# Moving sums, squares and scales of an encoder block's branch, output and attention stages

## The chip, the core and the metric

The kernel runs on one core of a Trainium2 chip. The core has five engines, each with its own queue of instructions that it works through in order: TensorE (PE, matrix products), VectorE (DVE), ScalarE (ACT), GpSimd (POOL) and SyncE (SP, which here only issues DMAs). An engine stops at an instruction whose inputs or buffers are not ready, and everything behind it in that queue stops too. The metric is the time of one launch in microseconds, as the median of several runs.

## The reference

The program is one block of a bidirectional encoder on 1024 tokens of width 1024, in float32:

```python
h = layer_norm(x, ln0_g, ln0_b)
proj = h @ w_in + b_in
qa, ka, va, qb, kb, vb, ga, gb = split(proj)
y_na  = neighbourhood_attention(qa, ka, va, rpb) @ w_branch_na    # 8 heads of 64
y_swa = windowed_gqa_with_sink(rotary(qb), rotary(kb), vb, sink) @ w_branch_swa
mixed = sigmoid(ga) * y_na + sigmoid(gb) * y_swa
h = layer_norm(ALPHA * h + mixed @ w_out + b_out, ln1_g, ln1_b)
u = square(relu(h @ w_ff1 + b_ff1))                               # width 4096
h = layer_norm(ALPHA * h + u @ w_ff2 + b_ff2, ln2_g, ln2_b)
```

The neighbourhood attention looks at a window of 8 rows by 16 columns on a 16 by 64 grid, the windowed one at 128 positions to each side, with a sink logit in the denominator.

## The kernel before

**Planes.** PE works in float16. Every operand of a large product is held as two float16 planes, a high one (the scaled value rounded) and a low one (what the rounding left). A product is the sum of three: high times high, high times low, low times high. So that the planes use the range of float16, each weight matrix and activation is scaled by a power of its own sum of squares. Such a scale takes a chain over four engines: ACT squares and accumulates (`square_sum`, `wo_square`, `b_square`, `mx_square`, `squares1`), PE adds the 128 partial sums with a tiny product against ones (`total_of` at L193, `wo_scale` at L1400, `mx_scale` at L1482, `sum_sq1`), DVE bounds the sum, POOL raises it to a power. Then ACT writes the high plane and DVE the low one (`b_split`, `wo_split`, `split_mx`, `head_hi` and `head_lo`).

**Stages**, by the time in the profile of before:

- 0 to 48 us: layer norm 0 in eight groups of 128 tokens (`ln0_norm`), transposition through PE (L385), evacuation as planes (`ln0_turn`), and the first gate projections (L429).
- 48 to 95 us: projections. Work on the weights of coming chunks is put into a list with `defer(n, ...)`, and `flush` issues those pieces whose n products have passed; `pump(n)` issues n projection products. The plan's four numbers per chunk say after how many products each part of a chunk's weight work is due.
- 95 to 393 us: 64 attention steps (`steps`). A step issues the scores of step s + 2 (`part_a`, whose first score bank is `score_ps[0]`, and DVE's reduction at L781), the low plane and the DMA transposition (pt) of step s + 1 (`part_l`), the exponential (`part_e`) and the products with the values (`part_c`, L887). Between them it pumps projection products in three parts, 12 in all per step up to about 217 us and 18 later. The sums of a weight chunk are written beside the scores, into `score_ps[0]` (`total_bank`). `evac2` adds the second half of a head's output on DVE.
- 393 to 463 us: the remaining gates in a scheme of seven block products (L1174), with `o_hi` and `o_lo` making the planes of the attention output (L1276, L1278).
- 463 to 556 us: the branch stage. For f from 0 to 7 and for each half of the tokens, `branch(f, half)` runs two groups of twelve products (neighbourhood, then windowed) into two PSUM tiles, DVE multiplies each with a gate, and POOL adds the two into `mx`. Around it, the next weights are loaded, squared, scaled and split, and two gates a half are loaded by SP and put through a sigmoid on ACT.
- 556 to 655 us: output products. For each group g of 128 tokens `out_mm` runs 24 products for each half of the width (L1610 to L1612), `out_evac` adds the residual, `ln1_norm` normalises, `turn` transposes it through PE (L1640), `turn_evac` and `combine` make the planes for the next stage. `late(g)` scales and shifts late residuals on POOL (zl, L1792). `head_w`, `squares1`, `sum_sq1`, `scale1`, `head_hi` and `head_lo` get the first weights of the next stage ready (hS, tw).
- 655 to 949 and 949 to 1240 us: the two layers of the MLP (L1779, L2255), seven block products each.

**What sets the order.** The program is a manual schedule: each engine's queue is what the program text issues to it, in the order of the text. Moving a call moves all its instructions on every engine. Each PSUM tag (mm, s, t, o) has two tiles.

Of the kernel before, what the change touches and what calls it, by code (L numbers as in the profile page):

```python
# [70 lines left out]
NO_DVE = ()  # L71
# [4 lines left out]
N_PRE = 188  # L76
WARM = 18, 4, 4, 2, 0, 2
# [15 lines left out]
def encoder_block(ctx, tc, x, w_in, w_br, w_out, w_ff1, w_ff2, par, rows, rpbp,  # L93
# [623 lines left out]
    def plan():  # L717

        def to(j, n):
            return lambda: got[j].to(n)  # L720
        ev = []
        for j in range(1, len(todo)):
            u = 48 * j
            t = (u - 112, u - 84, u - 44, u - 28) if j > 8 else \
                [200 + 40 * (j - 7) + x for x in (0, 24, 44, 64)] if j > 6 else \
                [20 * j - 24 + x for x in ((0, 14, 30, 34) if j > 1 else (0, 10, 24, 28))]
            if j > 8:
                ev.extend((u - 152 + 6 * x, 0, (j, x)) for x in range(4))
            elif j > 2:
                ev.append((max(20 * (j - 3) + 12, 2) + (30 if j > 6 else 0), 0, (j, None)))  # L730
            ev.extend((x, n, j) for x, n in zip(t, (1, 3, 4, 5)))
        for x, n, j in sorted(ev, key=lambda e: e[0]):
            if n == 0:
                defer(x, lambda j=j: fetch(*j))
            else:
                defer(x, to(j, n), pe=n == 3, only=n != 3)
# [124 lines left out]
    def part_c(s):  # L861
# [26 lines left out]
        if t % 2 == 1:  # L888

            oo = oT[o_row:o_row + 64, o_chunk, (t // 2) * 512:(t // 2 + 1) * 512]  # L890

            def evac():
                ACT.copy(oo, po[64:P, :])

            def evac2():
                DVE.tensor_tensor(out=oo, in0=po[0:64, :], in1=oo, op=ALU.add)  # L896
            if s == 63:
                last_evac.extend((evac, evac2))
            else:
                evac()  # L900
                if t == 3 and o_row == 64:
                    defer(14, evac2, 2, lambda: norm(o_chunk))
                else:
                    defer(14, evac2)
# [31 lines left out]
    with tc.manual_schedule(engines=MANUAL):  # L936
# [110 lines left out]
        def steps(s, n, before_b=None, before_c=None):  # L1047
# [21 lines left out]
            if s >= C_LAG:  # L1069
                part_c(s - C_LAG)  # L1070
            flush()
            pump(part[2])
# [334 lines left out]
        def wo_split(k):  # L1407
# [13 lines left out]
                9: ((b_split, 0),), 10: ((b_scale, 1),)}  # L1421
# [10 lines left out]
        for n, (p, i) in enumerate(gseq[2:], 2):  # L1432
# [13 lines left out]
            if n in (4, 5, 6, 7, 10, 11):  # L1446
# [3 lines left out]
                o_lo(n_o)  # L1450
                n_o += 1
        b_split(1)
# [26 lines left out]
        def mx_scale(half, ps, ones_, pw_):  # L1479
            DVE.tensor_reduce(out=mtot[:, half:half + 1], in_=msq[:, 8 * half:8 * half + 8], axis=mybir.AxisListType.X,  # L1480
                              op=ALU.add)
            PE.matmul(ps[:, 0:2], ones_, mtot[:, half:half + 1].to_broadcast([P, 2]), start=True, stop=True)  # L1482
# [29 lines left out]
        def branch(f, half, between=None):  # L1512
            both = []
            for gi, (act, tag) in enumerate(((o_na, "t"), (o_swa, "o"))):
                ps = psum(tag)
                gemm3(ps, bws[f], lambda part, k: act(part, k, half), nk=4, k0=4 * gi)
                if gi == 0 and between:
                    between()
                s_ = sg[f, gi, half]
# [8 lines left out]
        for f in range(8):  # L1528
            for half in range(2):
# [6 lines left out]
                else:  # L1536
                    if f + 2 < 8:
                        wo_load(f + 2)
                    if f + 1 < 8:
                        wo_scale(f + 1)  # L1540
                        if f:
                            b_split(f + 1)
# [4 lines left out]
                if half == 0:  # L1547
                    if f + 1 < 8:
                        wo_square(f + 1)
# [4 lines left out]
                branch(f, half, (lambda: mx_scale(0, psum("s"), ones_b, pwb)) if (f, half) == (7, 1) else None)  # L1554
# [3 lines left out]
        split_mx(0)  # L1558
# [45 lines left out]
    def out_mm(g, n, k0, k1):  # L1604
# [3 lines left out]
        ps, (mh, ml) = pss[g, n], mhl[g]  # L1608
        for k in range(k0, k1):
# [186 lines left out]
    with tc.manual_schedule(engines=MANUAL):  # L1796
# [10 lines left out]
        for g in range(NCG):  # L1807
# [5 lines left out]
            out_evac(g, 0)  # L1813
            out_mm(g, 1, 0, 4)
            if g:
                turn(g - 1)
            if g == 7:
# [17 lines left out]
            if g == 5:  # L1835
                head_split(0, 1)
                head_split(0, 2)
            if g == 6:
                for p in range(2, 4):
                    squares1(p, raws[p])  # L1840
            out_evac(g, 1)
            ps = bound_sum() if g == 0 else None
            ln1_norm(g)
            if g == 0:
                bound(ps)
            if g == 1:
                mx_scale(1, psum("o"), ones, pw)
# [702 lines left out]
```

## Time and profile before

| what | us |
|---|---|
| median of 3 runs | 1252.29 (1251.12 to 1252.44) |
| profiled execution | 1251.06 |
| its span | 1249.2 |
| PE busy in it | 1215.4 |
| DVE, ACT, POOL busy | 970.9, 870.9, 339.2 |

The span runs from the first to the last instruction of the core; the profiled execution's own time is 1.9 us longer. A row of the view of waits names the waiting engine, the tile and line of the waiting instruction, and the instruction that ended the wait. In rows of the timeline, the brackets hold the idle time of the engine just before, with its releaser. In the views a tile's name stands for all its buffers: `bc<-raw` at L1396 is `wo_square`, `mx` at L1523 is the sum of two gated halves, `sn` at L1881 the evacuation of the first MLP layer.

### The profile page before, as it was taken

To read this page: it belongs to the slowest core of one execution; us is meant where nothing else is said; L and a number is where in the kernel's file an instruction comes from. 1 tells how busy PE (TensorE), PEld (TensorE's weight loads), DVE (VectorE), ACT (ScalarE), POOL (GpSimd) and SP (SyncE) were. 2 spreads that over 40 slices of the span, in tenths; PEclk is the share of its full clock that TensorE was granted. 3 is DMA by queue.
4 is the path that set the end of the run, shared out by engine and by line. 5 is a ranking of instruction groups with operands and counts; after the bars stand their busy time and mean duration, and the time that the engine had idled before them with its cause. 6 is when DMAs were issued, how large, how long until landed. Compare 5 with 4: busy or idle time off the path is not lost.

```text
span 1249.2 us, 17241 instructions
## 1 busy us (share of the span) xinstructions
PE 1215.4 (97%) x6070; PEld 607.5 (49%) x6070; DVE 970.9 (78%) x1416; ACT 870.9 (70%) x1417; POOL 339.2 (27%) x368
## 2 busy tenths in 40 slices
PE   7999999999999998999999999999999999999997
PEld 5545555555555443444544444444444444444443
DVE  6788998878887974554678887877857777898888
ACT  7569889999876477753557877787776746344447
POOL 5202223434320014556621013432300002211207
PEclk9999999999999998999999999999999999999999
DMA  8654668686756335526333457776636635363333
GB/s 321 192 183 120 152 150 173 160 189 152 157 148 187 109 132 179 192 91 246 118 135 110 151 179 259 238 234 243 207 113 256 219 135 227 126 261 127 127 110 135
DMA packets 177878, 216.84 MB, mean 174 GB/s; under 512 B 111744, under 2 KB 125312, under 8 KB 171136
## 3 DMA queue, kind: packets, MB, share of 16 engines
q1 hardware_dynamic: 176816, 214.89, 54.2%
q8 instruction: 47, 0.77, 0.3%
q10 hardware_dynamic: 976, 0.87, 0.2%
q14 instruction: 39, 0.32, 0.1%
HBM read 130.69 MB, written 59.33 MB: 152 GB/s over the span
## 4 chain that ended last, share of the span: by engine, by line
PE 82%; ACT 7%; DVE 6%; issue 2%; DMA 2%; POOL 1%; POOLq 0%; SPq 0%; ACTq 0%; DVEq 0%
PE ps_mm L429 17%; PE ps_t L1779 6%; PE ps_o L1779 6%; PE ps_mm L2255 6%; PE ps_s L2255 6%; PE ps_mm L1779 6%; PE ps_t L2255 5%; PE ps_o L2255 5%; PE ps_s L1779 2%; PE ps_o L887 2%; PE ps_o L1174 2%; PE ps_mm L1174 1%; PE ps_t L1174 1%; PE ps_t L419 1%; PE ps_o L419 1%
## 5 line engine op out<-in xcount | busy, mean ns | idle before, releaser
L429 PE MATMUL ps_mm<-hT 128*128 128x512 f16 x960 | 226.4, 379 | 4.2 <-DVE hT L398 2.0
L1779 PEld LDWEIGHTS <-tw 128*128 128x128 f16 x1248 | 122.0, 99 | 146.0 <-issue 1.9
L2255 PEld LDWEIGHTS <-hS 128*128 128x128 f16 x1008 | 98.7, 98 | 118.2
L429 PEld LDWEIGHTS <-hT 128*128 128x128 f16 x960 | 90.6, 99 | 101.5 <-issue 12.0
L800 ACT ACTIVATE ss<-ss,sk 128x384 f32<-128x384 f32 (+1 forms) x128 | 73.8, 578 | 25.1 <-DVE sk L781 24.8
L1779 PE MATMUL ps_t<-hS,tw 128*128 128x512 f16 x384 | 88.1, 379 | 1.2 <-ACT sn L1881 1.1
L1971 DVE TENSOR_TENSOR usl<-usl 128x512 f32<-128x512 f32 x64 | 51.5, 804 | 23.5 <-ACT usl L1899 23.3
L429 PE MATMUL ps_mm<-hT,wpair 128*128 128x512 f16 x288 | 68.8, 380 | 0.0
L1700 POOL TENSOR_TENSOR c<-c 128x2 f32<-128x2 f32 x16 | 15.5, 974 | 194.7 <-DVE c L1699 194.7
L2275 POOL TENSOR_TENSOR acc<-acc,rst 128x512 f32<-128x512 f32 x16 | 31.8, 1986 | 122.7 <-DMA rst<-xr_d 114.8
L200 POOL TENSOR_TENSOR hT<-hT 128x2 f32<-128x2 f32 x30 | 25.2, 840 | 117.7 <-DVE hT L199 117.7
L2088 DVE SCALAR_TENSOR_TENSOR hS<-stg,c,hS 128x2048 f16<-128x2048 f32 x21 | 50.0, 2379 | 7.6 <-ACT hS L2085 7.6
L1706 DVE SCALAR_TENSOR_TENSOR tw<-raw,c,tw 128x512 f16<-128x512 f32 x60 | 51.8, 864 | 5.1 <-ACT tw L1703 4.8
L2255 PEld LDWEIGHTS <-hA 128*128 128x128 f16 x336 | 32.9, 98 | 39.6
L1174 PEld LDWEIGHTS <-hT 128*128 128x128 f16 x336 | 32.8, 99 | 39.6 <-issue 1.1
L887 PE MATMUL ps_o<-pt,vv 128*128 128x256 f16 (+1 forms) x448 | 49.1, 250 | 1.5 <-DVE oT L896 0.8
L812 DVE SCALAR_TENSOR_TENSOR pl<-ss,pl 128x768 f16<-128x768 f32 (+1 forms) x42 | 46.6, 1110 | 0.9 <-ACT pl L803 0.7
L887 PEld LDWEIGHTS <-vv 128*128 128x128 f16 x448 | 35.5, 98 | 18.6 <-DVE oT L896 2.0
L1779 PE MATMUL ps_o<-hS,tw 128*128 128x512 f16 x192 | 44.0, 379 | 0.0
L1703 ACT ACTIVATE tw<-raw,c 128x512 f16<-128x512 f32 x60 | 41.7, 708 | 2.8 <-DVE raw L1744 2.8
L1523 POOL TENSOR_TENSOR mx<-sg 128x512 f32<-128x512 f32 x16 | 30.1, 1881 | 49.8 <-DVE sg L1521 23.8
L587 POOL TENSOR_TENSOR bm<-tb,mk 128x128 f32<-128x128 f32 x56 | 42.9, 796 | 0.7
(431 smaller groups left out, 3082.2 us busy)
## 6 DMA issues: line engine op xcount, KB each, us to landing
us_d<-usl SPq DMA_DIRECT2D x112, 256.0 KB, 3.1
stg<-us_d SPq DMA_DIRECT2D x28, 1024.0 KB, 4.8
raw<-in_w_ff SPq DMA_DIRECT2D x24, 512.0 KB, 5.6
sg<-sg_d SPq DMA_DIRECT2D x32, 256.0 KB, 2.8
hA<-in_w_ff SPq DMA_DIRECT2D x8, 1024.0 KB, 7.6
hS<-in_w_ff SPq DMA_DIRECT2D x8, 1024.0 KB, 7.8
hT<-in_w_in SPq DMA_DIRECT2D x60, 128.0 KB, 2.5
hT<-in_w_in SPq DMA_DIRECT2D x11, 512.0 KB, 4.6
```

Of the source, the lines that this page charges most:

```text
L429: PE.matmul(ps, a[:, k, :], act(b, k), start=(k == 0 and i == 0), stop=(k == NK - 1 and i == 2))
L587: bias_ops.append(lambda o=o, g0=g0, m=m, g=g: POOL.tensor_tensor(out=bm[:, o + g * P:o + (g + 1) * P].rearrange("p (a c) -> p a c", c=8), ...
L800: ACT.activation(p, p, AF.Exp, bias=nm[:, i:i + 1], scale=-1.0, accum_out=sums_l[o_chunk][:, hh, 2 * t + i:2 * t + i + 1])
L812: DVE.scalar_tensor_tensor(out=pl[:, n:2 * n], in0=e[:, 0:n], scalar=P_SCALE, in1=pl[:, 0:n], op0=ALU.mult, op1=ALU.subtract)
L887: PE.matmul(o, vs, move(part), start=(m == 0 and part == 0), stop=(m == len(runs) - 1 and part == 1))
L1174: PE.matmul(ps, w[:, a, k, :], act[:, b, k, :], start=(first and k == 0 and m == 0), stop=(k == 3 and m == 2), skip_group_check=True)
L1703: ACT.activation(hi_lo(slot, 0), src, AF.Copy, bias=0.0, scale=w_scale(p))
L1706: DVE.scalar_tensor_tensor(out=hi_lo(slot, 1), in0=src, scalar=w_scale(p), in1=hi_lo(slot, 0), op0=ALU.mult, op1=ALU.subtract)
L1779: PE.matmul(ps, ww, act[:, part, k, :], start=(first and k == 0 and m == 0), stop=(k == 3 and m == 2), skip_group_check=True)
L1971: DVE.tensor_tensor(out=out, in0=a, in1=b, op=op)
L2088: DVE.scalar_tensor_tensor(out=slot[:, :, 1, :], in0=src, scalar=scale, in1=slot[:, :, 0, :], op0=ALU.mult, op1=ALU.subtract)
L2255: PE.matmul(ps, st[:, a, part, j * P:(j + 1) * P], w[:, a, wpart, :], start=(first and a == 0 and m == 0), stop=(a == 3 and m == 2), skip_ ...
```

## The change

Eight places are edited; no arithmetic is added or removed except that two normalisations go to another engine.

1. `NO_DVE` holds 2 and 3: the normalisations of two groups of layer norm 0 run on DVE, not on ACT.
2. In the projections' plan the weight sums are due 18 products after their start, not 14.
3. In an attention step the deferred list is emptied of what needs no PE before the last pumped products, and of the rest after them; before, all of it was emptied ahead of them. `evac2` is due after 12 products, not 14 (`D_E2`).
4. `wo_square(1)` is issued in the stage before the branch stage. `wo_scale(f + 1)` is issued between the two groups of products of `branch(f, 1)`, not before them, and `b_split(f + 1)` therefore ahead of it. `o_lo(6)` and `o_lo(7)` are issued after their loop.
5. `split_mx(0)` is issued inside the last branch, ahead of its second gate product, and the first output products run all those with the high plane of the activation first.
6. The sum over `msq` for the second half of `mx` and its scale are issued inside group 1 of the output stage, not at its end.
7. In group 6 the two `squares1` come after the normalisation, not before.

```diff
-NO_DVE = ()
+NO_DVE = 2, 3
+D_E2 = 12
...
-                [20 * j - 24 + x for x in ((0, 14, 30, 34) if j > 1 else (0, 10, 24, 28))]
+                [20 * j - 24 + x for x in ((0, 18, 30, 34) if j > 1 else (0, 10, 24, 28))]
...
-                    defer(14, evac2)
+                    defer(D_E2, evac2)
...
                 part_c(s - C_LAG)
+            flush(False)
+            pump(part[2])
             flush()
-            pump(part[2])
...
-                9: ((b_split, 0),), 10: ((b_scale, 1),)}
+                9: ((b_split, 0),), 10: ((b_scale, 1),), 11: ((wo_square, 1),)}
...
                 o_hi(n_o)
-                o_lo(n_o)
+                if n < 10:
+                    o_lo(n_o)
                 n_o += 1
+        o_lo(6)
+        o_lo(7)
...
+        def mx_sum(half):
             DVE.tensor_reduce(out=mtot[:, half:half + 1], in_=msq[:, 8 * half:8 * half + 8], axis=mybir.AxisListType.X,
                               op=ALU.add)
+
+        def mx_scale(half, ps, ones_, pw_):
+            if half == 0:
+                mx_sum(0)
...
                 if gi == 0 and between:
                     between()
+                if (f, half, gi) == (7, 1, 1):
+                    split_mx(0)
...
-                    if f + 1 < 8:
-                        wo_scale(f + 1)
-                        if f:
-                            b_split(f + 1)
+                    if f and f + 1 < 8:
+                        b_split(f + 1)
...
-                    if f + 1 < 8:
+                    if 2 <= f + 1 < 8:
                         wo_square(f + 1)
...
-                branch(f, half, (lambda: mx_scale(0, psum("s"), ones_b, pwb)) if (f, half) == (7, 1) else None)
+                branch(f, half, None if half == 0 else (lambda f=f: wo_scale(f + 1)) if f < 7 else
+                       (lambda: mx_scale(0, psum("s"), ones_b, pwb)))
...
-        split_mx(0)
         split_mx(1)
...
+        if (g, n) == (0, 0):
+            for k in range(8):
+                for x in range(2):
+                    PE.matmul(ps, mh[:, k, :], wo[:, x, k, ns], start=(k + x == 0), stop=False)
+            for k in range(8):
+                PE.matmul(ps, ml[:, k, :], wo[:, 0, k, ns], start=False, stop=(k == NK - 1))
+            return
...
             out_evac(g, 0)
+            if g == 1:
+                mx_sum(1)
             out_mm(g, 1, 0, 4)
             if g:
                 turn(g - 1)
+            if g == 1:
+                mx_scale(1, psum("o"), ones, pw)
...
+            out_evac(g, 1)
+            ps = bound_sum() if g == 0 else None
+            ln1_norm(g)
             if g == 6:
                 for p in range(2, 4):
                     squares1(p, raws[p])
-            out_evac(g, 1)
-            ps = bound_sum() if g == 0 else None
-            ln1_norm(g)
...
-            if g == 1:
-                mx_scale(1, psum("o"), ones, pw)
```

How the queues change is shown at three places; the change's lines have moved by up to 18, and a number behind "x" counts equal instructions in a row. The first is ACT's queue where the branch stage starts. `bc<-raw` is `wo_square`, `bc<-braw` is `b_square`, `wb` is a high plane of branch weights, `sg` are sigmoids and `wo` a high plane of output weights. Before:

```order
L1246 ACTIVATE go<-ps_mm,hT 128x512
L1278 CAST oS<-oT 128x1024
L1388 ACTIVATE wb<-braw,bc 128x1024
L1508 ACT_TABLE_LOAD
L1508 ACTIVATE sg<-sg,prm 128x512 x2
L1409 ACTIVATE wo<-raw,bc 128x1024
L1508 ACTIVATE sg<-sg,prm 128x512 x2
L1396 ACTIVATE bc<-raw 128x1024
L1374 ACTIVATE bc<-braw 128x1024
```

With the change:

```order
L1248 ACTIVATE go<-ps_mm,hT 128x512
L1398 ACTIVATE bc<-raw 128x1024
L1280 CAST oS<-oT 128x1024
L1390 ACTIVATE wb<-braw,bc 128x1024
L1517 ACT_TABLE_LOAD
L1517 ACTIVATE sg<-sg,prm 128x512 x2
L1411 ACTIVATE wo<-raw,bc 128x1024
L1517 ACTIVATE sg<-sg,prm 128x512 x2
L1376 ACTIVATE bc<-braw 128x1024
```

The square of wo(1) has gone ahead of the last plane of the attention output.

The second is PE's queue at one attention step: the products with the values (L887), the sum of a weight chunk (`ps_s<-hT`) and the four pumped products, of which the first is shown. Before:

```order
L887 LDWEIGHTS vv
L887 MATMUL ps_o<-pt,vv 128x256
L193 MATMUL ps_s<-hT 128x2
L429 LDWEIGHTS wpair
L429 MATMUL ps_mm<-hT,wpair 128x512
```

With the change, from the last of the four on:

```order
L430 LDWEIGHTS wpair
L430 MATMUL ps_mm<-hT,wpair 128x512
L194 MATMUL ps_s<-hT 128x2
L780 MATMUL ps_s<-kh,q 128x384
L781 MATMUL ps_s<-kl,q 128x384
```

The sum now stands behind the four products and right ahead of the next scores.

The third is ACT's queue in group 6 of the output stage. `z<-z,mv` is the normalisation, `junk<-hS` are the two `squares1`, the casts into hS are high planes from `combine`. Before:

```order
L1651 ACTIVATE mx<-ps_t,c_5477 128x128 x6
L1689 ACTIVATE junk,c_5477<-hS_6064 128x2048
L1689 ACTIVATE junk,c_5477<-hS_6065 128x2048
L284 ACTIVATE z<-z,mv 128x1024
L1656 CAST hS_6065<-s2t 128x4x128
```

With the change:

```order
L1667 ACTIVATE mx<-ps_t,c_5477 128x128 x6
L285 ACTIVATE z<-z,mv 128x1024
L1705 ACTIVATE junk,c_5477<-hS_6064 128x2048
L1705 ACTIVATE junk,c_5477<-hS_6065 128x2048
L1672 CAST hS_6065<-s2t 128x4x128
```

The normalisation passes both squares; the casts keep their place behind them.

More of the change, by code (lines that the diff above doesn't have):

```diff
@@ L901, in part_c @@
                 if t == 3 and o_row == 64:
-                    defer(14, evac2, 2, lambda: norm(o_chunk))
+                    defer(D_E2, evac2, 2, lambda: norm(o_chunk))
                 else:
-                    defer(14, evac2)
+                    defer(D_E2, evac2)
     def fills():
@@ L1477, in mx_square @@
                            saturate=False)
-        def mx_scale(half, ps, ones_, pw_):
+        def mx_sum(half):
             DVE.tensor_reduce(out=mtot[:, half:half + 1], in_=msq[:, 8 * half:8 * half + 8], axis=mybir.AxisListType.X,
                               op=ALU.add)
+        def mx_scale(half, ps, ones_, pw_):
+            if half == 0:
+                mx_sum(0)
             PE.matmul(ps[:, 0:2], ones_, mtot[:, half:half + 1].to_broadcast([P, 2]), start=True, stop=True)
```

## The prediction

> **What bounds the kernel now.** I read the page's first lines, then everything that TensorE (PE) waits for, and last the stretches around its longest waits.
>
> ```profile
> span 1249.2 us, 17241 instructions
> PE 1215.4 (97%) x6070; PEld 607.5 (49%) x6070; DVE 970.9 (78%) x1416; ACT 870.9 (70%) x1417; POOL 339.2 (27%) x368
> ```
>
> PE is busy for 97% of the span, and the change removes none of its products. So only the 33.8 us in which PE is not busy, and time in which it is busy at a lower clock, can move. The view of waits (engine, operation and line, what released it: total us, times, longest) names the holes:
>
> ```profile
> PE ps_s L1400 <- ACT bc L1396: 4.3, 1, 4.3
> PE ps_s L193 <- DVE sk L781: 2.8, 3, 1.2
> PE ps_t L1640 <- ACT z L284: 2.1, 1, 2.1
> PE ps_o L1482 <- DVE prm L1480: 2.1, 1, 2.1
> PE ps_mm L1612 <- DVE m L1495: 1.6, 1, 1.6
> PE ps_o L887 <- DVE oT L896: 0.8, 1, 0.8
> PE ps_o L887 <- DMA pt<-hT: 0.7, 1, 0.7
> PE ps_t L193 <- ACT hT L222: 0.7, 1, 0.7
> PE ps_o L385 <- ACT ln L368: 0.2, 1, 0.2
> ```
>
> The edits touch the work around all of these. Windows (length, busy time and instruction count of PE, PEld, DVE, ACT and POOL, then granted clock, DMA share, GB/s) show where a hole also cost clock, and how full VectorE (DVE) is in attention:
>
> ```profile
> 125.00:150.00 25.00, 23.76 (x145) 14.46 (x144) 23.37 (x44) 19.52 (x40) 6.35 (x9) 1.00 0.65 159
> 150.00:175.00 25.00, 23.81 (x147) 14.35 (x144) 22.96 (x44) 20.87 (x48) 7.76 (x11) 1.00 0.62 146
> 217.00:393.00 176.00, 176.00 (x1016) 101.84 (x1015) 142.26 (x287) 150.26 (x294) 60.93 (x76) 1.00 0.67 158
> 470.00:475.00 5.00, 1.94 (x6) 1.01 (x7) 2.76 (x4) 4.97 (x9) 1.48 (x2) 0.73 0.70 245
> 475.00:480.00 5.00, 5.00 (x15) 1.87 (x14) 0.75 (x1) 3.47 (x6) 0.78 (x2) 0.59 0.63 210
> 650.00:655.00 5.00, 5.00 (x22) 2.74 (x21) 4.93 (x9) 3.53 (x9) 0.00 (x0) 0.68 0.26 105
> ```
>
> **The branch stage: the largest term.** The chain of waits (start us, length us, what) into the 4.3 us hole reads, with a stretch of undisturbed products ahead of it for the pace:
>
> ```profile
> 96.22 2.60 PE ps_mm L429 x12
> ...
> 470.65 1.32 ACT sg L1508 x2
> 471.97 1.05 ACT bc L1396 x2
> 473.06 0.59 PE ps_s L1400 x2
> ```
>
> The wait is for wo_square(1) (bc at L1396), queued on ScalarE (ACT) behind the sigmoids of loaded gates and a weight split. It now stands before the stage, so this release is gone; and wo_scale(f+1) goes in after the twelve products of one half instead of ahead of them. Behind the hole the clock cost 5 × (1 − 0.73) + 5 × (1 − 0.59) = 3.4 us of full-speed time; about 0.4 of it fell into the hole itself, so 3.0 were paid. Undisturbed, a product takes 2.60 / 12 = 0.216 us. Gross gain 4.3 + 3.0 = 7.3 us.
>
> [...]
>
> What is late next is ACT itself (start, length, operation, and idle before it with its releaser):
>
> ```profile
> 480.07 1.06 ACT L1396 ACTIVATE bc<-raw 128x1024 fp8e5<-128x1024 f32 x1 [1.13 <-DMA raw<-in_w_out]
> 484.80 0.63 ACT L1476 ACTIVATE bc<-mx 128x512 fp8e5<-128x512 f32 x1 [2.40 <-POOL mx L1523]
> 485.46 1.15 ACT L1388 ACTIVATE wb<-braw,bc 128x1024 f16<-128x1024 f32 x1
> ```
>
> With PE 7.3 us earlier, these do not all follow: the load of raw(2) stays where it was (its buffer is freed by a split behind the same loads), so wo_square(2) still starts near 480.1; behind it stand another such square (to 482.4), that of mx(0,1) (0.63), and the high plane of wb(2) (1.15), to 484.3; its low plane on DVE takes some 1.3 us more (the splits at L1495 below), to 485.6. PE starts f = 2 at 468.8 + 3 × 24 × 0.216 = 484.4 (three halves after the hole's beginning, 473.06 − 4.27), and wants that plane at its third product, 484.8. I take a new wait of 0.8 us, from 0 to 1.5 (the row's length either way). Net −6.5, range −7.3 to −5.8.
>
> **Attention.** The sums (L193) write beside the scores of the current step, so they wait until DVE has reduced those scores:
>
> ```profile
> 142.10 0.61 DVE L781 CUSTOM_DVE_ANT_0 ss<-ps_t,bd,snk 128x384 f32<-128x384 f32 x1
> ```
>
> Moving them behind the step's last four pumped products gives 4 × 0.216 = 0.86 us of cover. The two waits of 1.2 fall to 0.4, the third (2.8 − 2 × 1.2 = 0.4) vanishes: −2.1. The release of evac2 (the 0.8 us at L896) by 12 products instead of 14 falls into the step before, which takes that wait away. Against this, all pieces that an emptying of the deferred list issues (scale pieces on DVE and POOL, ACT splits, weight loads on SP) now stand in front of the next step's scores rather than in the middle of the step, on a DVE that is 94% and 92% busy in these windows. PE already waited 0.7 us for a transposed probability tile (pt), which comes at the end of a chain through DVE; a DVE piece of 0.5 to 0.8 us in front of a reduction makes some pt that much later. I take one or two such waits, +0.7. Net −2.2; from −3.6 (everything goes) to +3 (five new waits of the size seen, 1.2 us, against the whole gain of 2.9). The shift of the weight sums in the projections by 14 to 18 products covers 4 × 0.216 = 0.86, more than the 0.7 us at L193 ps_t: −0.7.
>
> **Layer norm.** Two normalisations go from ACT to DVE:
>
> ```profile
> L366 DVE TENSOR_SCALAR ln<-ln,mv x1: 814/814/814, 12.4 to 12.4; 128x1024 f32<-128x1024 f32 x1
> 28.37 1.24 ACT L368 ACTIVATE ln<-ln,mv 128x1024 f32<-128x1024 f32 x1
> 28.97 0.69 DVE L398 TENSOR_TENSOR hT<-t,hT 128x512 f16<-128x512 f32 x1
> ```
>
> On ACT the last ended at 29.6, just as PE came for it (the 0.2 us wait). On DVE it stands behind the low plane that ends at 29.66, so it ends near 30.45: +0.8, less a little because ACT, relieved of 2.5 us, evacuates earlier: +0.7, from −0.5 to +1.0.
>
> **First output products.** The 1.6 us wait at L1612 is for the low plane of m:
>
> ```profile
> 557.42 3.48 DVE L1495 SCALAR_TENSOR_TENSOR m<-mx,mxc,m 128x1024 f16<-128x1024 f32 x2
> ```
>
> The chain of waits gives the first of these two splits 1.3 us. Sixteen high-plane products first are 16 × 0.216 = 3.5 us of cover: −1.6. The last gate product of the branch on DVE (0.6 to 0.8 us) now stands behind the first split, and so, later by that, do POOL's last sum of two gates, ACT's last square and what SP loads behind it; I found no use of them that is due within 3 us, and if there is one the gain is smaller by 0.7. From −1.8 to −1.0.
>
> **The output stage.** Here I do not credit the waits. The 2.1 us at L1482 is taken off PE, but the next stretches hang on GpSimd (POOL):
>
> ```profile
> 583.15 0.71 POOL L1485 TENSOR_TENSOR mxc<-mxc,c 128x2 f32<-128x2 f32 x1
> 583.82 12.03 POOL L1792 TENSOR_TENSOR zl<-zl 128x512 f32<-128x512 f32 x8
> 596.03 0.55 POOL L1629 TENSOR_TENSOR mv<-mv,mhalf 128x1 f32<-128x1 f32 x1 [0.18 <-DVE mv L1628]
> ```
>
> Twelve microseconds of late residual work start behind mv(1) and end where mv(2) is wanted; I take it that each group's normalisation then follows the one before at POOL's pace as far as transposition 5, since four more additions stand between each two. What leaves POOL's path is the power for mxc, 0.7 us, which now runs in POOL's idle time before mv(1). So PE gains 2.1 and waits 1.3 of it later: −0.8.
>
> ```profile
> 635.76 0.83 PE ps_t L1640 x7
> 636.59 9.38 DMA hS<-in_w_ff
> 648.06 1.13 ACT z L284
> 690.87 2.75 PE ps_t L1779 x12
> ```
>
> The rows of POOL and ACT ahead of z:
>
> ```profile
> 644.24 0.35 POOL L282 TENSOR_SCALAR mv<-mv 128x1 f32<-128x1 f32 x1
> 643.56 1.91 ACT L1689 ACTIVATE junk<-hS 128x2048 fp8e5<-128x2048 f32 x1 [3.74 <-DMA hS<-in_w_ff]
> 646.05 1.91 ACT L1689 ACTIVATE junk<-hS 128x2048 fp8e5<-128x2048 f32 x1 [0.49 <-DMA hS<-in_w_ff]
> ```
>
> In this chain no PE work stands between 636.59 and 690.87: a load started by transposition 5, the squares of what it brings, z, then ACT and DVE pieces end to end. Moving the squares behind z removes the wait at L1640, but both squares are still ahead of the next casts. The first had run while its data came in (from 643.56); now it starts after z, whose scale POOL has ready at 644.6, so near 644.6 + 1.1 = 645.7. Two of 1.9 end near 649.6, and the casts start 0.4 later than at 648.06 + 1.13 = 649.2. The sums of squares on PE then wait about 2 us in place of the transposition. For 690.87 that is about +0.5, and the clock dip at 650 stays. Both together −0.3; if all of it were PE's, 2.1 + 2.1 + 1.6 of clock = −5.8.
>
> **Sum.** −6.5 − 2.2 − 0.7 + 0.7 − 1.6 − 0.3 = −10.6 us. The profiled execution took 1251.06 us (span 1249.2); the median of the runs is 1252.29, 1.2 above it. 1251.1 − 10.6 = 1240.5, or 1241.7 on the scale of the median.
>
> **Rivals.**
> A: the output stage gives its waits to PE, because POOL's late work slips behind what it blocks and z, not the squares, sets the casts. For it: L1640 waits on z by name. Against: both squares remain before the casts. 1241.7 − 5.5 = 1236.2; chance 0.15. [...]
> B: DVE's queue in attention gives nothing back, or takes some: net +1 instead of −2.2, 1245. For it the 94%; against, from 217 to 393 us, with 18 products a step, PE is busy for all of 176.00 us. Chance 0.2.
> C: the branch hole moves instead of closing. If one more wait of the 2.40 us that the square of mx(0,1) shows comes between wo_square(2) and wb(2), PE stands for 0.8 + 2.4 at the start of f = 2, and such a hole costs clock as the 2.1 us one did (5 × 0.32 = 1.6): 1241.7 + 4.0 = 1245.7; chance 0.12. Against: that wait was for PE's own sums, and PE now comes earlier.
> D, slower: every one of the some 30 steps before 217 us loses time because the emptied list stands before the reductions on a full DVE. The other terms give −8.4, so it decides above 0.28 us a step; at 0.4 us it is +12.0, together +3.6: 1255.9. For it: the DVE share and the pt wait; against: PE had slack enough for only three waits of this kind in those steps. Chance 0.05.
> The forecast itself has 0.48. Its own range is 1239 to 1244.
>
> **How the numbers follow.** 1234.5 holds A and some luck, 1248 holds B and C with their spread; outside lie D and half the tails, about 2 in 10. About 0.2%, 2.5 us, is what a measurement can tell here. Faster by more: all but D and the bad ends of B and C, 0.89; within it 0.06; slower 0.05.
>
> **What would show it.** Right: no L1400 wait and a clock of 1.00 from 470 to 480; L193 waits of 0.4 or less; a new wait under 1.5 us for wb(2) at f = 2; no L1612 wait; a wait at transposition 5 (L1640's) of about 1.3; a wait of about 2 us at the sums of squares in the last output group, with the clock still dipping. Wrong: PE through the last output group without a hole (A), new pt or reduction waits spread over the steps before 217 us (B, D), or a hole over 3 us in the branch stage (C).

## The result

The change makes the kernel slower: 1258.78 us in the median of 4 runs (1256.27 to 1259.37) against 1251.7 for the kernel before (4 runs, 1250.88 to 1252.44), a ratio of 1.0053 with a 95% interval of 1.0035 to 1.007. The forecast was 1241.7, with 1234.5 to 1248. The profiled execution of the change, 1256.27 us, is the fastest of its four, so its trace shows somewhat less loss than the median.

The first lines of the page of the changed kernel:

```profile
span 1254.5 us, 17213 instructions
PE 1216.4 (97%) x6070; PEld 607.8 (48%) x6070; DVE 971.1 (77%) x1418; ACT 868.5 (69%) x1415; POOL 330.5 (26%) x368
```

All engines but GpSimd do as much work as before to within 0.3%, GpSimd 2.6% less, and the span is 5.3 us longer, so the loss is waiting. What TensorE waits for now, over the whole span (rows below 0.7 us and those that are much as before are left out):

```profile
PE ps_o L888 <- DMA pt<-pl: 3.8, 2, 3.1
PE ps_t L838 <- DVE sk L782: 2.2, 1, 2.2
PE ps_mm L430 <- ACT hT L700: 2.2, 2, 1.1
PE ps_o L888 <- DMA pt<-hT: 2.1, 1, 2.1
PE ps_t L1656 <- ACT z L285: 2.0, 2, 1.6
...
PE ps_o L1710 <- ACT junk L1705: 1.7, 1, 1.7
PE ps_s L194 <- DVE sk L782: 1.6, 2, 1.3
...
PE ps_o L386 <- DVE ln L367: 0.9, 1, 0.9
...
PE ps_t L422 <- DVE wb L1391: 0.7, 1, 0.7
```

The waits that the change aimed at outside attention are gone, or nearly: 0.2 us is left for the weight scale in the branch stage (4.3 before), and there is no row for the split at the first output products (1.6) or for the scale of the second half of mx (2.1). In their place stand the first four rows, all of attention; before, only the fourth of them had a row, of 0.7. The same piece of work in both traces, by its start, tells where the time went (us from the span's start):

| place | before | changed | difference |
|---|---|---|---|
| products with the values, step 0 | 100.99 | 101.58 | +0.6 |
| the same, step 30 | 225.79 | 238.31 | +12.5 |
| the same, step 63 | 393.16 | 405.98 | +12.8 |
| end of the wait at the first scale of mx, end of the branch stage | 553.72 | 560.54 | +6.8 |
| end of the last wait at the start of the next stage (L1779) | 690.87 | 695.83 | +5.0 |
| span | 1249.2 | 1254.5 | +5.3 |

Behind attention the change gains 7.8 us, near the forecast; in the first 30 steps it loses 12. The steps' differences jump at few places, not in every step: +0.6 at step 1, +2.5 at step 6, +4.3 over steps 9 to 11, +4.7 over steps 17 to 19, −2.3 at steps 27 and 28 (where the waits of 0.8, 0.7 and 0.4 of before are gone), +1.9 at step 30. The first two windows, around steps 9 to 11 and 17 to 19, show holes and clock; the other two are the start of the branch stage, some 13 us later than before:

```profile
125.00:150.00 25.00, 20.89 (x115) 12.46 (x116) 21.09 (x37) 17.37 (x38) 7.06 (x10) 0.93 0.61 142
175.00:200.00 25.00, 20.80 (x116) 12.23 (x115) 21.42 (x43) 21.19 (x47) 3.70 (x6) 0.93 0.60 138
480.00:485.00 5.00, 5.00 (x26) 2.43 (x25) 2.69 (x3) 4.97 (x7) 0.00 (x0) 1.00 0.96 297
485.00:490.00 5.00, 5.00 (x26) 2.44 (x25) 3.10 (x7) 4.17 (x8) 3.24 (x4) 1.00 0.31 93
```

In the first two TensorE is busy for 20.9 and 20.8 of 25 us, at a mean clock of 0.93 (25 × 0.07 = 1.7 us of full-speed time in each window). VectorE is *less* busy than before in the first of them (21.1 against 23.4): it is not overfull, it stands. What it stands for, from 95 to 235 us, in the largest rows, first in the kernel before, then in the changed one:

```profile
DVE ss L781 <- PE ps_s L780: 8.5, 11, 1.4
DVE kl L568 <- ACT q L561: 5.4, 3, 2.1
DVE pl L812 <- ACT pl L803: 0.7, 1, 0.7
```

```profile
DVE q L682 <- ACT q L677: 9.4, 6, 2.5
DVE sl L832 <- ACT sk L827: 4.9, 2, 3.3
DVE qs L628 <- ACT qf L620: 4.7, 2, 2.5
DVE pl L813 <- ACT pl L804: 2.4, 2, 2.1
```

Before, VectorE waited mostly for TensorE's scores, which costs nothing: it was ahead. Now it waits for ScalarE, with the next scores' reductions behind it in its queue. The longest single wait is at step 30:

```profile
233.60 0.18 DVE L832 TENSOR_TENSOR sl<-sl,sk 128x16 f32<-128x16 f32 x1 [3.29 <-ACT sk L827]
```

This adds the sink's exponential to the sums of a chunk. ScalarE makes that exponential (L827, from 233.09) behind a weight square and the exponentials of a step's scores. The reductions follow at 233.98, and TensorE stood 1.3 us at the sum (L194). The largest row is L682. The place of its longest wait, ScalarE's rows first, then VectorE's, in the changed kernel:

```profile
131.43 0.60 ACT L677 CAST q<-qf 64x512 fp32r<-64x512 f32 x1
134.63 0.61 ACT L677 CAST q<-qf 64x512 fp32r<-64x512 f32 x1 [2.60 <-PE ps_t L781]
136.65 0.61 ACT L801 ACTIVATE ss<-ss,sk 128x384 f32<-128x384 f32 x1 [1.41 <-DVE sk L782]
```

```profile
132.06 0.68 DVE L682 TENSOR_TENSOR q<-qf,q 64x512 fp32r<-64x512 f32 x1
135.27 0.69 DVE L682 TENSOR_TENSOR q<-qf,q 64x512 fp32r<-64x512 f32 x1 [2.52 <-ACT q L677]
135.99 0.62 DVE L782 CUSTOM_DVE_ANT_0 ss<-ps_s,bd,snk 128x384 f32<-128x384 f32 x1
```

This is the rotation of the next heads' queries: ScalarE's copy (L677) and VectorE's difference (L682) make their two planes. The second copy waits 2.6 us for TensorE's score products: the tile q has three buffers, and the one that it writes into is still read by the scores of the current head until 134.59. ScalarE stands at that copy, VectorE at the difference behind it, and the reductions of scores that TensorE had finished near 131 begin at 135.99. No run here tries a fourth buffer; the one with the rotation a step later, below, moves the copy instead. The exponentials, the low plane, the DMA transposition and the product with the values follow late by as much: the 2.1 and 3.1 us at L888, the 1.1 at L700.

Why the rotation comes earlier can be read from the code. Its pieces stand in the deferred list: the evacuation when a projection's products have been issued, the shuffle 4 products later, and then one piece at each step's scores. The fourth of these products is the last of a step. Before, the list was next looked at behind the following scores; the changed kernel looks at it at once, so the whole chain begins a step sooner. That is not part of what the edit's few words say (sums at the end of a step): the second `flush()` takes all pieces that are due.

### The profile page after: what moved, and what is told of

Read it like the earlier page. It is cut to its first block, busy times and chain, and to the rows that moved or that the text cites. A ratio compares the mean times of both kernels' runs of the same rounds, so it can differ in the third digit from the quotient of the medians.

```text
span 1254.5 us, 17213 instructions
## 1 busy us (share of the span) xinstructions
PE 1216.4 (97%) x6070; PEld 607.8 (48%) x6070; DVE 971.1 (77%) x1418; ACT 868.5 (69%) x1415; POOL 330.5 (26%) x368
## 4 chain that ended last, share of the span: by engine, by line
PE 71%; DVE 11%; ACT 8%; issue 3%; POOL 3%; DMA 1%; SPq 0%; POOLq 0%; DVEq 0%; ACTq 0%
PE ps_mm L430 13%; PE ps_t L1795 6%; PE ps_o L1795 6%; PE ps_s L2273 6%; PE ps_mm L2273 6%; PE ps_mm L1795 6%; PE ps_t L2273 5%; PE ps_o L2273 5%; PE ps_s L1795 2%; PE ps_o L888 2%; PE ps_o L1176 2%; PE ps_mm L1176 1%; PE ps_t L1176 1%; ACT ss L801 1%; PE ps_o L420 1%
## 5 line engine op out<-in xcount | busy, mean ns | idle before, releaser
L201 POOL TENSOR_TENSOR hT<-hT 128x2 f32<-128x2 f32 x30 | 29.7, 989 | 150.9 <-DVE hT L200 150.9
L888 PE MATMUL ps_o<-pt,vv 128*128 128x256 f16 (+1 forms) x448 | 49.1, 250 | 5.9 <-DMA pt<-pl 3.8
L888 PEld LDWEIGHTS <-vv 128*128 128x128 f16 x448 | 35.7, 98 | 23.0 <-issue 6.7
L2273 PE MATMUL ps_mm<-hA,hS 128*128 128x512 f16 x192 | 42.9, 379 | 0.0
L2273 PE MATMUL ps_s<-hA,hS 128*128 128x512 f16 x192 | 42.7, 379 | 0.0
```

Source lines behind the costliest of these rows:

```text
L888: PE.matmul(o, vs, move(part), start=(m == 0 and part == 0), stop=(m == len(runs) - 1 and part == 1))
L2273: PE.matmul(ps, st[:, a, part, j * P:(j + 1) * P], w[:, a, wpart, :], start=(first and a == 0 and m == 0), stop=(a == 3 and m == 2), skip_ ...
```

## The experiments

In each group the runs were timed against the kernel before on the same chip; its median there was 1251.9, 1254.28, 1251.71 and 1251.31 us, so groups are compared by ratios and by places in the traces.

### Attention alone, and everything else alone

The kernel before with only the attention edit:

```diff
-                    defer(14, evac2, 2, lambda: norm(o_chunk))
+                    defer(12, evac2, 2, lambda: norm(o_chunk))
...
-                    defer(14, evac2)
+                    defer(12, evac2)
...
-            flush()
-            pump(part[2])
+            flush(False)
+            pump(part[2])
+            flush()
```

> The kernel before with the attention edit alone (the list emptied of non-PE pieces, then the last pumped products, then the rest; evac2 due after 12). If the loss lies in this edit: the 12.2 us that the trace of the change has lost between step 0 and step 30 appear alone, 1251.7 + 12 = about 1264. If it lies in the layer-norm or plan edits, or in how the edits act together: within 3 us of 1251.7.

1265.64 us, ratio 1.0113 (1.0096 to 1.013): +13.7 us. In its trace step 30 is 13.9 us late.

The change with this edit undone:

```diff
-D_E2 = 12
+D_E2 = 14
...
-            flush(False)
-            pump(part[2])
-            flush()
+            flush()
+            pump(part[2])
```

> The change without the attention edit (list emptied as before, evac2 due after 14). If the loss lies there and the rest is as the trace shows it (+0.6 by step 0, -8.0 from step 63 to the end): 1251.7 - 7.4 = about 1244.3. If the other edits lose too: above 1250.

1244.73 us, ratio 0.9945 (0.993 to 0.996). The loss lies in the attention edit alone; all the rest together is a gain of 7 us.

### The rotation a step later

```diff
-        defer(0, evac, late[0], turn)
+        defer(0, evac, 6 if in_steps else late[0], turn)
```

> The change with one number more: within the steps the first piece of a rotation is due 6 products after its evacuation, not 4, so that it isn't taken at the end of a step but in the middle of the next, as in the kernel before. Theory 1 (the rotations start a step early, so the copy into the q buffer comes before that buffer's last scores, and ScalarE and VectorE stand for 2.5 us at the head of their queues): the two clusters at steps 9 to 11 and 17 to 19 go, 4.3 + 4.7 us, 1258.8 - 9 = about 1250. Theory 2 (VectorE is full, and any piece ahead of the reductions costs, whichever it is): within 2 us of 1258.8.

1247.4 us, ratio 0.9967 (0.9954 to 0.998): 11.4 us less than the change, for one number. The copies and differences at the same place, in this run:

```profile
130.44 1.26 ACT L677 CAST q<-qf 64x512 fp32r<-64x512 f32 x2
```

```profile
131.76 1.40 DVE L682 TENSOR_TENSOR q<-qf,q 64x512 fp32r<-64x512 f32 x2
```

They run without a pause, a step later in the program. The loss at step 6 is gone too (there the shuffle, L628, waited 2.45 us for its evacuation). So it isn't that *any* piece ahead of the reductions costs: the reductions still follow shuffles, copies and sums here. What costs is a piece whose own input or buffer isn't ready. What is left, 2.7 us more than without the attention edit, are waits of 0.4 to 1.4 us between steps 13 and 30, of this kind:

```profile
PE ps_s L194 <- DVE sk L782: 2.7, 3, 1.4
PE ps_t L838 <- DVE sk L782: 2.0, 2, 1.4
```

In this run VectorE waits at the addition of the sink's exponential (L832, for sk of L827) three times, for 1.98 us at 153.75, 1.69 at 188.39 and 3.29 at 224.59; step 30 is again 2.1 us late. That these make up the rest fits the trace, but no run takes them out alone.

### Layer norm and plan alone

The kernel before with:

```diff
-NO_DVE = ()
+NO_DVE = 2, 3
...
-                ... ((0, 14, 30, 34) if j > 1 else ...
+                ... ((0, 18, 30, 34) if j > 1 else ...
```

> The kernel before with the two normalisations on VectorE and the weight sums due after 18 products, nothing else. By the trace of the change (a wait of 0.95 for 0.18, and the 0.66 us wait in the projections gone) +0.1 to +0.6: 1252. If these two edits bring the loss into attention: above 1255.

1253.33 us, ratio 1.0007 (0.9998 to 1.0016), step 63 at +0.56. The wait of 0.95 at the transposition is there, and the one of 0.66 in the projections is gone; but a wait of 0.70 of a sum for the scores' reductions has come at step 1.

### Only what begins on TensorE

The second look at the list takes sums and transpositions alone:

```diff
+    def flush(pe=True, early=False, rest=True):
...
-            if e[0] <= 0 and (pe or not e[2]) and (...)
+            if e[0] <= 0 and (pe or not e[2]) and (rest or e[2]) and (...)
...
             flush(False)
             pump(part[2])
-            flush()
+            flush(True, False, False)
```

> The change with the second emptying of a step's list cut down to the pieces that begin on TensorE (sums and transpositions); all other pieces keep the places they had in the kernel before. Theory 1 (what costs is the pieces of the list that come along, above all the rotations): the sums' waits at L193 fall as predicted, without new holes, 1244.7 (the change without the attention edit) - 2 to 3 = about 1242. Theory 2 (work of any kind behind the last products and ahead of the reductions costs, the sums' own scale pieces on VectorE too): above 1246.

1247.62 us, ratio 0.9946 (0.9927 to 0.9965). The ratio is that of the run without the edit, but the kernel before was unquiet in this group (1252.28 to 1256.84), so the traces decide: step 63 comes at 398.09 against 393.93 without the edit. The run is 4 us worse, not 2 to 3 better. The sums' waits have not fallen:

```profile
PE ps_s L194 <- DVE sk L782: 4.1, 4, 1.9
```

By their place they begin 0.9 us later, as they should, but the reductions end later by as much. VectorE's rows there, first in this run, then in the one with the normalisation later (below):

```profile
137.88 1.78 DVE L813 SCALAR_TENSOR_TENSOR pl<-ss,pl 128x640 f16<-128x640 f32 x1
141.42 1.41 DVE L859 SCALAR_TENSOR_TENSOR oT<-oT,vs,rb 128x512 f32<-128x512 f32 x2 [1.76 <-DMA rb<-rl_d]
142.75 0.61 DVE L782 CUSTOM_DVE_ANT_0 ss<-ps_s,bd,snk 128x384 f32<-128x384 f32 x1
```

```profile
139.59 0.62 DVE L782 CUSTOM_DVE_ANT_0 ss<-ps_s,bd,snk 128x384 f32<-128x384 f32 x1
...
142.36 1.40 DVE L859 SCALAR_TENSOR_TENSOR oT<-oT,vs,rb 128x512 f32<-128x512 f32 x2
```

The normalisation of a head's output (L859) needs reciprocals that are transposed on TensorE (L838), stored, and loaded back as rb. The transposition had moved half a step later along with the sums, and the normalisation had not. There are three stalls of this shape: 1.76 us at step 10 (above), 2.35 at step 19 and 2.27 ahead of step 27.

### The sums alone; and the normalisation later

Two ways around it. First, the second look takes only the weight sums, the transpositions keep their old place, and `evac2` is due after 14:

```diff
-D_E2 = 12
+D_E2 = 14
...
+    def flush(pe=True, early=False, rest=True):
...
-            if e[0] <= 0 and (pe or not e[2]) and (...)
+            if e[0] <= 0 and (pe or not e[2]) and (rest or e[2] == 'sum') and (pe != 'turn' or e[2] != 'sum') and (...)
...
-                defer(x, to(j, n), pe=n == 3, only=n != 3)
+                defer(x, to(j, n), pe='sum' if n == 3 else False, only=n != 3)
...
-            flush(False)
+            flush('turn')
             pump(part[2])
-            flush()
+            flush(True, False, False)
```

> The change, with only the weight sums behind the last products of a step; the transpositions of the reciprocals and all other pieces of the list keep the places of the kernel before, and evac2 is due after 14. Theory 3 (in the run before, the sums' own move was paid for by the reciprocals: their transposition came half a step later, so VectorE stood 1.8 and 2.4 us at the normalisation for their reload, ahead of the reductions): the waits at L193/L194 of 1.24 fall to 0.4 and the small ones go, 2.3 us less than the change without the attention edit: 0.9945 - 0.0018 = about 0.993 of the kernel before. Theory 2 (anything behind the last products delays the next scores): 0.9945 or more.

1243.29 us, ratio 0.9931 (0.9918 to 0.9943). The row of the sums' waits:

```profile
PE ps_s L194 <- DVE sk L782: 0.7, 2, 0.4
```

Two waits of 0.4, as the prediction's arithmetic had it (1.24 less the cover of 0.86). The places in the trace show a smaller gain than the ratio does: against the change without the attention edit, step 30 comes 1.4 us earlier, but step 63 only 0.7 (393.23 against 393.93). What takes the rest back behind step 30, in pieces of about 0.1, stays open.

Second, the run of the section above, in which sums and transpositions are taken last, with the normalisation 14 products behind `evac2`:

```diff
-                    defer(D_E2, evac2, 2, lambda: norm(o_chunk))
+                    defer(D_E2, evac2, 14, lambda: norm(o_chunk))
```

> The run with only the pieces that begin on TensorE moved (sums and transpositions), and the normalisation of a chunk due 14 products after evac2, not 2. Theory 3: VectorE no longer stands for the reload of the reciprocals, and the holes at steps 10, 19 and 20 (1.3 + 1.9 us, and 1.7 of clock) shrink to 0.4 each: 3 to 4 us less than that run, 0.9946 - 0.0028 = about 0.992 of the kernel before. If the reload isn't the cause: within 1 us of it, 0.994 to 0.9955.

1242.44 us, ratio 0.9927 (0.9914 to 0.9941). Step 63 comes at 392.18 against 398.09, 5.9 us earlier by one number, where 3 to 4 were expected. No row of L194 is left; steps 11 and 19 gain 1.4 us each over before. With the holes went a stretch of half clock at 178.5; the mean clock is 0.997 against 0.996. What remains is a wait for a pt transposition and one for a sum's scale ahead of a transposition, with a loss of 1.6 us at step 30:

```profile
PE ps_o L888 <- DMA pt<-hT: 2.1, 1, 2.1
PE ps_t L838 <- DVE hT L200: 1.1, 1, 1.1
```

### The branch stage alone

The kernel before with the change's edits of that stage:

```diff
-                9: ((b_split, 0),), 10: ((b_scale, 1),)}
+                9: ((b_split, 0),), 10: ((b_scale, 1),), 11: ((wo_square, 1),)}
...
+        o_lo(6)
+        o_lo(7)
...
-                        wo_scale(f + 1)
...
+                branch(f, half, None if half == 0 else (lambda f=f: wo_scale(f + 1)) if f < 7 else
```

> The kernel before with the edits of the branch stage alone (square of wo(1) earlier, wo_scale between the two products, o_lo(6) and o_lo(7) after their loop). Prediction's step: 1251.9 - 6.5 = about 1245.4, by the trace of the change -6.1 and a wait of 0.7 for the low plane of wb(2). If the gain depends on what else was changed: less than 4.

1244.26 us, ratio 0.9922 (0.9905 to 0.9939). This is the group in which the kernel before was unquiet, so again the trace decides: the end of the branch stage comes at 547.15 where it was at 553.72, 6.6 us earlier. Its waits from 465 to 560 us:

```profile
PE ps_mm L1614 <- DVE m L1498: 1.6, 1, 1.6
PE ps_t L421 <- DVE wb L1389: 0.7, 1, 0.7
PE ps_s L1485 <- DVE prm L1483: 0.5, 1, 0.5
```

The new wait of 0.7 is for the low plane of wb(2), at f = 2.

### The output stage, edit by edit

Three runs with one edit more or less, read by the time from the end of the branch stage to the end of the wait at the next stage's start. It was 553.72 to 690.87 = 137.15 in the kernel before, 136.91 in the run with the branch's edits alone, and 135.28 in the change without attention.

The change without attention, with the squares ahead of the normalisation again:

```diff
+            if g == 6:
+                for p in range(2, 4):
+                    squares1(p, raws[p])
             out_evac(g, 1)
             ps = bound_sum() if g == 0 else None
             ln1_norm(g)
-            if g == 6:
-                for p in range(2, 4):
-                    squares1(p, raws[p])
```

> The change without the attention edit, and without the squares' move (the two squares ahead of the normalisation of group 6 again). Prediction's step (the squares set the next casts either way, so the move costs about 0.5): 1244.7 - 0.5 = about 1244.2, with the wait of 1.65 at the sums gone and one of about 2 at the transposition back. Rival (the removed wait was TensorE's, 2.1 and 1.6 of clock): 1244.7 + 3.7 - 1.65 = about 1246.8 or more.

1244.96 us, ratio 0.9926 (0.9908 to 0.9944); 135.71 for the stretch, so the squares' move gains 0.4. The wait at the transposition is back with 3.07 us, not about 2.

The change without attention, with the sum and scale of the second half of mx at the end of group 1 again:

```diff
-            if g == 1:
-                mx_sum(1)
             out_mm(g, 1, 0, 4)
...
-            if g == 1:
-                mx_scale(1, psum("o"), ones, pw)
...
             if g == 0:
                 bound(ps)
+            if g == 1:
+                mx_sum(1)
+                mx_scale(1, psum("o"), ones, pw)
```

> The change without the attention edit, and with the sum and scale of the second half of mx at the end of group 1 again. Prediction's step (POOL sets the pace up to transposition 5, only 0.7 to 0.8 us leaves its path): 1244.7 + 0.8 = about 1245.5, with a wait of about 2 at that sum and the later ones at the transpositions and the output products gone. Rival (the wait was TensorE's): 1246.8.

1246.57 us, ratio 0.9937 (0.992 to 0.9954); 135.99, so this move gains 0.7, of a wait of 2.1.

The kernel before with the branch's edits and those of the first output products:

```diff
+                if (f, half, gi) == (7, 1, 1):
+                    split_mx(0)
...
-        split_mx(0)
...
+        if (g, n) == (0, 0):
+            for k in range(8):
+                for x in range(2):
+                    PE.matmul(ps, mh[:, k, :], wo[:, x, k, ns], start=(k + x == 0), stop=False)
+            for k in range(8):
+                PE.matmul(ps, ml[:, k, :], wo[:, 0, k, ns], start=False, stop=(k == NK - 1))
+            return
```

> The kernel before with the branch stage's edits and the first output products' (the split of mx(0) earlier, high planes first), nothing else. In the run with the branch's edits alone, TensorE went from the end of the branch (546.6) to the last wait of the next stage's start (683.0) in 136.4 us. Prediction's step (the wait of 1.6 is TensorE's): 134.8, and the time falls by 1.6. If POOL, ScalarE and VectorE set the pace of the whole output stage, as the sums by differences suggest: 135.7 to 136, and the time falls by 0.4 to 0.7.

1243.7 us, ratio 0.9938 (0.9924 to 0.9953); 136.07, so the removed wait of 1.6 is worth 0.8 where it was to be worth 1.6. The three differences, 0.8 + 0.7 + 0.4, add up to 1.9; all three together make 137.15 − 135.28 = 1.9 from the kernel before, or 136.91 − 135.28 = 1.6 from the run with the branch's edits. Over the four traces with the old output stage the stretch is 136.7 to 137.15, so each difference from it is good to a few tenths. In this run's trace, unlike that of the branch's edits alone, a stretch of half clock stands behind the wait of 2.07 us at the second scale (575.3 to 578.7; the mean clock of the two traces is 0.996 against 0.998). It does not hide a larger gain: the run with only the second scale moved back has this edit and the squares' move, no such stretch, and 136.91 − 135.99 = 0.9 for the two.

That other engines set this stretch is seen best where TensorE's own time varies. The same wait of 1.65 at the sums of squares stands in the change without attention and in the run with the sums alone. Windows behind it, in the first, then in the second:

```profile
640.00:645.00 5.00, 3.35 (x16) 1.59 (x14) 2.47 (x4) 5.00 (x9) 0.00 (x0) 0.84 0.03 13
645.00:650.00 5.00, 5.00 (x20) 2.12 (x19) 4.90 (x12) 1.98 (x6) 1.37 (x2) 0.82 0.00 0
```

```profile
639.00:644.00 5.00, 3.35 (x20) 1.73 (x19) 2.58 (x5) 5.00 (x9) 0.00 (x0) 1.00 0.01 2
644.00:649.00 5.00, 5.00 (x25) 2.29 (x24) 4.90 (x11) 1.98 (x6) 1.37 (x2) 1.00 0.00 0
```

In the first the hole costs clock, 5 × 0.16 + 5 × 0.18 = 1.7 us. In the second it doesn't, and TensorE waits 1.6 us longer at the next transposition (L1656 for z). The stretch is 135.28 in the first, 682.57 − 547.25 = 135.32 in the second: 1.7 us of TensorE's time make no difference to it.

### Layer norm back on ScalarE

The run with the later normalisation, and:

```diff
-NO_DVE = 2, 3
+NO_DVE = ()
```

> The run with the later normalisation of a chunk (0.9927 of the kernel before), with the two normalisations of layer norm 0 on ScalarE again. Prediction's step (the move to VectorE costs 0.7): 0.9927 - 0.0006 = about 0.992, with a wait of about 0.2 at the transposition in place of 0.95. If ScalarE's relief pays for it: the same 0.9927.

1241.45 us, ratio 0.9919 (0.9903 to 0.9936). The wait at the transposition is 0.18 us against 0.95, and step 0 begins at 100.52 against 101.28: the move to VectorE costs 0.8. (Step 0 alone would not tell: it begins between 100.86 and 101.58 in the nine traces that have both this edit and the plan's.) This is the fastest kernel of the study, 10 us under the kernel before and 17 under the change.

## Why the prediction was wrong

**Attention: the step that failed.** The prediction had −2.2, with +3 as its bad end; it is +12.2 in the change and +14.0 alone, from step 0 to step 63. The wrong step is the sentence on the pieces that "now stand in front of the next step's scores": it priced each at its own duration ("a DVE piece of 0.5 to 0.8 us in front of a reduction makes some pt that much later") and took one or two. What a moved piece costs is not its duration but how long *it* waits, since everything behind it waits too: 2.5 us for a copy that waits for a buffer, 2.45 for an evacuation on another engine, 3.3 for a piece that ScalarE came to late; in the run with sums and transpositions alone, 1.8 to 2.4 for a reload. Rival D had the right place (the emptied list in front of the reductions) and the wrong mechanism: a full VectorE and a loss in every step. VectorE was less busy than before where the loss is largest, and the loss stood at a few places (steps 6, 9 to 11, 17 to 19 and 30); that its 1255.9 lies near the measured time is luck.

The arithmetic for the sums themselves was right (two waits of 0.4 in the run with the sums alone), and with the rotations and the reloads out of the way the kernel comes to 1242.4, near the 1241.7 that was forecast for the change. The totals agree better than the term, though: from step 0 to step 63 attention gains nothing in the run with the sums alone, and 1.3 us in the one with the later normalisation, not 2.2. The change as written, besides, starts the rotations a step sooner. The prediction did not follow the chain of due times behind the second look at the list (evacuation, 4 products, then one piece a step); the order of instructions shows the copies of q a step earlier, and `bufs=3` on the tile says that there they may have to wait for the scores.

**Plan: −0.7 came out as none.** The wait of 0.7 moved from the projections to step 1, where a shifted sum meets the first reductions. What covers it was counted, what it is moved past was not.

**Layer norm: right.** +0.7 forecast, 0.8 measured.

**Branch stage: right.** −6.5 forecast, −6.6 measured in the run with these edits alone, with the new wait for the low plane of wb(2) at 0.7 (forecast 0.8) and, there, a clock of 1.00 from 470 to 480. Rival C did not come.

**First output products: size off.** −1.6 forecast, −0.8 measured. The term was credited to TensorE in full, right ahead of the part that says that the next stretches hang on POOL; the same reasoning held for it.

**Output stage: small as forecast, the parts half right.** −0.3 forecast, −1.1 measured: the scale of the second half −0.8 and −0.7, the squares +0.5 and −0.4. The step that was wrong is that the later start of the squares delays what follows by its full 0.5; that TensorE would wait at the sums of squares instead (1.65, forecast about 2) was right. The wait of about 1.3 at transposition 5 came as 0.50 at the output products and 0.39 at a transposition, and behind that wait of 1.65 the clock dipped in the change without attention (0.84 and 0.82), but not in the change's own trace (1.00 from 650 to 660 us). Rival A (−5.8 in this stage) did not come.

Without attention the terms of the forecast add up to −8.4, and the change without it measures −7.2.

**The clock.** The prediction let a hole of 2.1 us cost clock, and some did: in the changed kernel the holes of 2.1 and 3.1 us in attention were each followed by a stretch of half clock (1.7 us of full-speed time), while behind the one of 2.2 us at step 6 the granted clock stayed at 1.00 (120 to 130 us).

```profile
144.68:148.09 3.41, 3.41 (x10) 1.93 (x9) 3.18 (x6) 2.37 (x6) 1.42 (x2) 0.50 0.51 128
182.23:185.64 3.41, 3.41 (x11) 1.92 (x10) 2.70 (x6) 2.84 (x7) 1.41 (x2) 0.50 0.40 97
```

In the kernel before, half clock stood from 649.78 to 653.20 us, behind the hole of 2.08 us at L1640; behind that of 2.07 us at L1482 the clock was 1.00 (580 to 590 us). Of the same hole of 1.65 us, one was followed by it and another was not (0.84 and 0.82 against 1.00 and 1.00 in the windows of the output stage above).

## What to carry to other kernels

When an edit changes *when a list of deferred work is looked at*, list every kind of piece in it and follow each chain of due times, not only the pieces that the edit is for; then ask of each moved piece what it waits for at its new place, since the price in an in-order queue is that wait, paid by everything behind it, and not the piece's duration (here 2.52 us of wait at L682, for a piece of 0.69). A busy share of 94% did not tell what VectorE would cost: before, it waited mostly for TensorE (8.5 us at L781), at no cost; in the change it was less busy (21.1 us against 23.4 from 125 to 150), and TensorE waited for it. So read what an engine waits for beside its share. A stretch that two or three engines pace in turn is to be recognised once and then for every edit in it: none of the waits that were taken off TensorE there was worth its own length.

## What was not expected of the hardware

The same hole of 1.65 us on TensorE, at the sums of squares, stands in eight of the traces, with the same instructions around it. What followed it differs: a granted clock of 0.84 and 0.82 in the change without attention, of 1.00 and 1.00 in the run with the sums alone (the windows above), and of 1.00 in the changed kernel:

```profile
650.00:655.00 5.00, 3.35 (x23) 2.26 (x21) 0.31 (x1) 4.97 (x7) 0.00 (x0) 1.00 0.26 108
655.00:660.00 5.00, 5.00 (x25) 2.25 (x23) 4.93 (x9) 3.49 (x9) 0.00 (x0) 1.00 0.00 0
```

The hole of 2.07 us at the second scale of mx stands in six traces. In the kernel before the clock was 1.00 behind it; in the run with the branch's edits and those of the first output products a stretch of half clock followed (575.3 to 578.7). What decides whether half clock follows such a hole, no run here shows.
